# A hybrid-attention layer: the last two latent heads by token halves, and three token tiles of the output projection among the last values

## The chip, the cores and the metric

The kernel runs on one core of one Trainium2 chip. The metric is the device time of one execution in microseconds (us), from the chip's own clock. The core has a matrix engine (TensorE, PE in the profile, with PEld for its weight loads), three elementwise engines (VectorE is DVE, ScalarE is ACT, GpSimd is POOL) and SyncE (SP), which here only issues DMA transfers. Every engine works through its own instruction list in the order in which it was written down, and waits on semaphores for the others. TensorE multiplies a 128-row stationary matrix by up to 512 moving columns and adds into PSUM, a memory of eight banks of 128 x 512 floats. The granted clock of TensorE that the profile shows is a share of its full speed.

## The reference

The kernel computes one encoder layer for 1024 tokens of width 1024, in float32. What matters here is the end of the mixer and the beginning of the channel part:

```python
q = rmsnorm(...); k = rmsnorm(...)          # 8 latent heads, q and k of 96, v of 64
o_mla = mla_attention(q, k, v)              # chunk-causal: a 64-token chunk sees all chunks up to its own
o_ca = chunk_attention(cq, ck, cv, rel_bias)  # 8 band heads of 64, a band of 9 chunks
mixed = jnp.dot(jnp.concatenate([o_mla, o_ca], axis=-1), w_out)
x = x + g_a[:, None, :] * mixed
h = modulate(rmsnorm(x, g_mlp_norm), sh_m, sc_m)
u = causal_dwconv(jnp.dot(h, w_up), conv_w, conv_b)
gate, val = jnp.split(u, 2, axis=-1)
x = x + g_m[:, None, :] * jnp.dot(jax.nn.silu(gate) * val, w_down)
```

So the output projection of a 128-token tile needs the attention outputs of all 16 heads for those tokens, and the norm needs a whole row of the result.

## The kernel before, in words

**Precision.** A float32 product is made of three faster ones. Each operand is split into a high part and the remainder (hi_of, lo_of, lines 77 and 84): hi x hi, hi x lo and lo x hi are added in PSUM (lines 154 to 156, and 1075 to 1077 for the channel part).

**Attention.** The heads are worked through in units. A unit is one head and one half of the queries (g = 0 or 1, 512 tokens, four query tiles). There are 16 units of band heads and then 16 of latent heads, named by (group, head, half); the latent ones run in the order (group 0 or 1, head 0 to 3, half 0, 1). For each query tile, TensorE makes the scores (line 771) into a PSUM bank pair of the tag S, VectorE takes the row minimum (789, 790), ScalarE the exponential with its row sum (797), VectorE the reciprocal (799, 800), POOL the scaled high part (line 73) and VectorE the low part (819), both in 16 bits. SP then issues DMA transposes of them (831), and TensorE multiplies by the values (859). Values are done for two query tiles at a time, three tiles behind the scores (DEPTH). In the second half of a latent head a tile has 640 to 1024 keys, in the first 128 to 512. At the end of a unit ScalarE and VectorE divide and combine (868, 869) into a tile om, and SP stores it to oT_d in DRAM (873; for the last unit, the store is held and written down behind the first loads of the next stage, 871).

**Fillers.** Among the units the kernel runs independent work in small steps, paced by a debt of estimated cost (pace, fill_step, need). The last one, "oca" (f_oca), is the output projection of the band heads: it loads and splits half of w_out, makes a partial sum for each token tile ("oc", lines 154 to 156), and stores it to part_d. It is called to completion behind the last unit.

**Output projection.** load_wo loads (667) and splits the other half of w_out. o_load(t) loads the latent heads' outputs of a tile from oT_d (ol, line 1017), ScalarE makes the high part oh (77) and POOL the low part, in place in ol (84). For each tile, 24 matmuls go into a bank pair "op" of the pool psB; there are three such pairs. VectorE adds the partial sum pa (1134), multiplies by the gate gabc (1135) and adds x (1136); SP stores the result x1 (1137); ScalarE squares it (1138), POOL takes the reciprocal root (119, 120), and VectorE scales the row (1143). Loads of pa (1110), x (1114) and gabc (1117) come through SP, as do those of the first channel weights wu (1086), whose parts wa, wb, wd and wf ScalarE (77) and POOL (84) split. o_load(4) to o_load(7) each wait for a free buffer of a former tile.

**The channel part** starts with TensorE transposes of the normed rows (ht_ps, 1044; ScalarE, 1046, copies and modulates) and then builds sums of pages on VectorE (1172 to 1192), before its long run of matmuls from about 717 us.

**Order.** The program is written in the order above, but a list scheduler sets each engine's final order: it plays the instructions against estimated durations and takes high_priority offsets and issue_after (an instruction is written down behind another one) as its guides. The PSUM pool psA serves attention with the tags mm, S, T and others; psB, which has op and hT, is opened when psA is closed.

## Time and profile before

| | us |
|---|---|
| runs (three) | 1338.59, 1341.95, 1342.17 |
| median | 1341.95 |
| the profiled execution's own time | 1345.32 |
| its span, first to last instruction | 1343.5 |
| TensorE busy in the span | 1223.3 (91%) |
| VectorE busy | 1095.6 (82%) |
| ScalarE busy | 621.9 (46%) |
| POOL busy | 579.7 (43%) |
| mean granted TensorE clock | 0.948 |

The stages that matter, on the time axis of the profile: the last scores begin at 608.10, the last values at 621.17, the output projection's first matmul at 626.96 and its last at 674.05; the channel part's long run of matmuls starts at 717.5. Rows of the timeline give start, duration, engine, line, operation, and the tiles written and read, with the idle time of the engine in front and who ended it in square brackets. Rows of the chain give start, duration and the piece that the end of the program waited for. Shares of busy time are averages over stages with different limits, so the stretch of the change has to be read by itself.

### The profile page before, as it was taken

Reading aid. Unit: us, or ns where it says so; the run is one execution under the profiler, and the core shown is the slowest. Engines: PE = TensorE matmul, PEld = TensorE weight load, DVE = VectorE, ACT = ScalarE, POOL = GpSimd, SP = SyncE. Lnnn points to the kernel's source line nnn. Section 1 sums busy time; section 2 is a strip of 40 time slices with the busy share of each in tenths; the row PEclk is TensorE's granted clock in tenths of the full one; section 3 lists DMA queues with packets and bytes.
Section 4 is the critical chain, followed back from the end, with each engine's and each line's share of the span. In section 5 each row is a group of like instructions: output and inputs, shape, how many; then the busy total and the mean of one; then the engine's idle time right before and its main releaser. Section 6 shows DMA issues by size and latency. Waiting matters only on the chain.

```text
span 1343.5 us, 18697 instructions
## 1 busy us (share of the span) xinstructions
PE 1223.3 (91%) x6168; PEld 1002.6 (75%) x6168; DVE 1095.6 (82%) x1928; ACT 621.9 (46%) x1132; POOL 579.7 (43%) x610
## 2 busy tenths in 40 slices
PE   4899798998867798896988999999999999999998
PEld 3888587887655576774867888888888886888886
DVE  6977898864679987894989888899999997687667
ACT  4453555443556544552375444444434444433331
POOL 5474656565646763363725444444435431000000
PEclk9899798999797899997998999999999998999999
DMA  8415677944413486779901333333333326943441
GB/s 321 140 32 120 137 173 181 192 124 113 90 30 80 97 166 153 148 153 270 364 32 63 110 113 131 102 107 113 120 116 117 127 96 232 388 154 118 131 160 62
DMA packets 223689, 190.57 MB, mean 142 GB/s; under 512 B 148708, under 2 KB 166884, under 8 KB 223592
## 3 DMA queue, kind: packets, MB, share of 16 engines
q1 hardware_dynamic: 223592, 189.38, 49.5%
q8 instruction: 48, 0.79, 0.2%
q14 instruction: 49, 0.40, 0.1%
HBM read 117.24 MB, written 37.49 MB: 115 GB/s over the span
## 4 chain that ended last, share of the span: by engine, by line
PE 41%; DVE 10%; issue 3%; ACT 2%; DMA 1%; POOL 1%; SPq 0%; DVEq 0%; ACTq 0%; POOLq 0%
PE p L1075 7%; PE p L1077 7%; PE p L1076 7%; PE dnA_P L1404 2%; PE dnA_P L1406 2%; PE dnA_P L1405 2%; PE dnB_P L1406 1%; PE dnB_P L1405 1%; PE dnB_P L1404 1%; DVE u L1246 1%; DVE u L1247 1%; PE dnA L1404 1%; PE op L154 1%; PE dnA L1406 1%; PE dnA L1405 1%
## 5 line engine op out<-in xcount | busy, mean ns | idle before, releaser
L77 ACT ACTIVATE dnP<-dnr 128x1024 fp32r<-128x1024 f32 x73 | 77.5, 1064 | 117.1 <-PE dnA_P L1406 46.4
L1378 DVE TENSOR_TENSOR dnP<-dnr,dnP 128x1024 fp32r<-128x1024 f32 x72 | 87.9, 1223 | 52.5 <-ACT dnP L77 52.5
L73 POOL TENSOR_SCALAR hlm<-Pm,rim 128x512 f16<-128x512 f32 (+3 forms) x96 | 69.3, 732 | 79.8 <-DVE rim L800 21.8
L84 POOL TENSOR_TENSOR wf<-wu,wf 128x512 fp32r<-128x512 f32 x22 | 39.3, 1789 | 116.3 <-ACT wf L77 106.8
L1246 DVE SCALAR_TENSOR_TENSOR u<-c,cvp,u 128x1023 f32<-128x1023 f32 x44 | 65.0, 1519 | 27.8 <-ACT u L1245 27.8
L73 POOL TENSOR_SCALAR hlc<-Pc,ric 128x640 f16<-128x640 f32 (+2 forms) x64 | 49.7, 780 | 61.1 <-ACT Pc L797 15.4
L819 DVE SCALAR_TENSOR_TENSOR hlm<-Pm,rim,hlm 128x512 f16<-128x512 f32 (+3 forms) x96 | 66.7, 706 | 10.3 <-POOL hlm L73 10.1
L797 ACT ACTIVATE Pc<-sc,mc 128x640 f32<-128x640 f32 (+2 forms) x64 | 42.1, 658 | 53.5 <-DVE mc L786 30.6
L1245 ACT ACTIVATE u<-c,cvp 128x1024 f32<-128x1024 f32 x44 | 52.3, 1237 | 28.7 <-DVE c L1338 19.5
L84 POOL TENSOR_TENSOR wb<-wu,wb 128x512 fp32r<-128x512 f32 x22 | 38.5, 1751 | 61.6 <-ACT wb L77 55.5
L797 ACT ACTIVATE Pm<-sm,mm 128x128 f32<-128x128 f32 (+3 forms) x64 | 47.1, 736 | 38.4 <-DVE mm L790 21.1
L1247 DVE SCALAR_TENSOR_TENSOR u<-c,cvp,u 128x1022 f32<-128x1022 f32 x44 | 64.8, 1510 | 0.0
L859 PE MATMUL pvm<-PTm,vt 128*128 128x256 f16 (+1 forms) x320 | 46.6, 298 | 15.4 <-DMA PTm<-hlm 10.7
L819 DVE SCALAR_TENSOR_TENSOR hlc<-Pc,ric,hlc 128x640 f16<-128x640 f32 (+2 forms) x64 | 50.4, 790 | 8.8 <-POOL hlc L73 8.2
L154 PE MATMUL ipq<-wq_s,hT 128*128 128x256 f32 x192 | 56.1, 295 | 0.0
L155 PE MATMUL ipq<-wq_s,hT 128*128 128x256 f32 x192 | 56.0, 293 | 0.0
L859 PEld LDWEIGHTS <-vt 128*128 128x128 f16 x320 | 32.0, 110 | 31.5 <-DMA PTm<-hlm 15.0
L156 PE MATMUL ipq<-wq_s,hT 128*128 128x256 f32 x192 | 55.4, 289 | 0.0
L77 ACT ACTIVATE wc<-ws 128x512 fp32r<-128x512 f32 x21 | 13.3, 632 | 86.0 <-DVE ws L1094 86.0
L1406 PE MATMUL dnA_P<-dnP 128*128 128x512 f32 x132 | 51.3, 389 | 0.0
L1405 PE MATMUL dnA_P<-dnP 128*128 128x512 f32 x132 | 51.3, 389 | 0.0
L1404 PE MATMUL dnA_P<-dnP 128*128 128x512 f32 x132 | 51.2, 389 | 0.0
(434 smaller groups left out, 4429.6 us busy)
## 6 DMA issues: line engine op xcount, KB each, us to landing
wu<-w_up SPq DMA_DIRECT2D x44, 512.0 KB, 3.5
dnr<-g_d SPq DMA_DIRECT2D x73, 256.0 KB, 2.8
aw<-w_ada SPq DMA_DIRECT2D x48, 256.0 KB, 3.6
g_d<-u SPq DMA_DIRECT2D x22, 512.0 KB, 3.0
dnr<-w_down SPq DMA_DIRECT2D x44, 256.0 KB, 5.4
adaw<-w_ada_a SPq DMA_DIRECT2D x16, 512.0 KB, 6.5
x<-x SPq DMA_DIRECT2D x16, 512.0 KB, 9.0
g_d<-gs SPq DMA_DIRECT2D x22, 256.0 KB, 2.7
```

What stands on the lines that cost most here:

```text
L73: pool.tensor_scalar(o, i, s, 1.0, op0=MUL, op1=MUL)
L77: act.activation(o, i, AF.Copy)
L797: act.activation(pr[:, :n], sv, AF.Exp, bias=m[:], scale=-1.0, accum_out=rsum[:, 0:1])
L819: dve.scalar_tensor_tensor(hl[:, w:2 * w], pp, ri[:], hl[:, :w], op0=MUL, op1=SUB)
L859: last = pe.matmul(dst, u.vst(j), mov, start=(x == 0), stop=(x == len(todo) - 1), skip_group_check=True)
L1075: pe.matmul(pt, sh, pg[:, 0], start=(k == 0 and not add), stop=False, skip_group_check=skip)
L1076: pe.matmul(pt, sh, pg[:, 1], start=False, stop=False, skip_group_check=skip)
L1077: last = pe.matmul(pt, sl, pg[:, 0], start=False, stop=(k == 3), skip_group_check=skip)
L1378: r = f(*a, **k)
L1404: pe.matmul(pt, sh, w[:, 0, 0], start=start, stop=False, skip_group_check=add)
L1405: pe.matmul(pt, sh, w[:, 1, 0], start=False, stop=False, skip_group_check=add)
L1406: pe.matmul(pt, sl, w[:, 0, 0], start=False, stop=stop, skip_group_check=add)
```

## The change

Three things are changed together:

1. The last two latent heads are ordered by token halves: (2,0), (3,0), (2,1), (3,1) of group 1, where it was (2,0), (2,1), (3,0), (3,1). When (3,0) is done, all heads are finished for tokens 0 to 511, which are tiles 0 to 3 of the output projection. One key page of unit (1,3,1) moves into another buffer for it, and the stores of the last two units' outputs are both held and written down behind the first four ol loads.
2. The band heads' filler "oca" is called to completion in front of the last three score tiles (N_OCA) instead of behind all units, which also lets the other half of w_out be loaded and split earlier.
3. The products of tiles 0, 1 and 2 (op_product) go into banks of the attention's own pool: tile 0 into two banks of the tag mm, tiles 1 and 2 into pairs of the tag S. The last two query tiles' values, values(7), are written down behind the product of tile 1 (N_OP). psA is closed, and psB opened, behind the add of tile 2. The add of tile 0 is done in two halves.

In the instruction lists that come of it, ScalarE has the first three conversions oh in front of the exponentials of the last unit's tiles 6 and 7, and POOL the four low parts among that unit's high parts; VectorE has the adds of tiles 0, 1 and 2 in front of the x add of tile 0, and ScalarE the squares of x0 and x1 both in front of wa's conversion.

```diff
--- before.py
+++ after.py
@@ -38,6 +38,8 @@
 GRP = 2
 GSTEP, LAG = 2, 4
 NPRE = 10
+N_OCA = 3
+N_OP = 1
 DEPTH = 3
 OFF_S, OFF_P, OFF_V = 400, 200, 200
 P_BUFS, HL_BUFS, TB = 3, 4, 1
@@ -705,7 +707,7 @@
             act.activation(hi[:rows], pt[:rows], AF.Copy)
             dve.tensor_tensor(lo[:rows], pt[:rows], f32(hi[:rows]), op=SUB)
             return hi, lo
-        pg = at.tile([P, 2, 512], F32R, name=name, tag=tag, bufs=bufs)
+        pg = at.tile([P, 2, 512], F32R, name=name, tag=tag, bufs=bufs) if bufs else pgtile([P, 2, 512], F32R, name)
         act.activation(pg[:rows, 0], pt[:rows], AF.Copy, scale=gain)
         dve.scalar_tensor_tensor(pg[:rows, 1], pt[:rows], gain, f32(pg[:rows, 0]), op0=MUL, op1=SUB)
         return pg
@@ -867,7 +869,7 @@
                     inv = vscale[u.vs][1]
                     act.activation(dst[r0], u.pv[r1], AF.Copy, scale=inv[r1])
                     dve.scalar_tensor_tensor(dst[r0], u.pv[r0], inv[r0], dst[r0], op0=MUL, op1=ADD)
-                    if final:
+                    if u in units[-2:]:
                         held.append(lambda: sp.dma_start(u.dst_d[r0, u.g * 512:(u.g + 1) * 512], dst[r0]))
                     else:
                         anchor["om"] = sp.dma_start(u.dst_d[r0, u.g * 512:(u.g + 1) * 512], dst[r0]).ins
@@ -917,7 +919,7 @@
 
         def prep():
             q = qk_page(lambda j: mq[gr, (4 * g + j) // 2][:, j % 2, hh, :], f"mq{gr}{hh}_{g}", QK, "Q", 2, None)
-            k = qk_page(lambda j: mk[gr, (4 * g + j) // 2][:, j % 2, hh, :], f"mk{gr}{hh}_{g}", QK, "K", 3, gk_m[:QK])
+            k = qk_page(lambda j: mk[gr, (4 * g + j) // 2][:, j % 2, hh, :], f"mk{gr}{hh}_{g}", QK, "K", 0 if (gr, hh, g) == (1, 3, 1) else 3, gk_m[:QK])
             pages[gr, hh, g] = (q, k)
         u = Unit(f"m{gr}{hh}", 0, QK,
                  lambda: (pages[gr, hh, g][0], [pages[gr, hh, i][1] for i in range(g + 1)]),
@@ -979,9 +981,12 @@
             fill_step()
     first = [anchor["pe"]]
     units = [ca_unit(p, g, o) for p in range(4) for g in range(2) for o in range(2)]
-    units += [mla_unit(gr, hh, g) for gr in range(2) for hh in range(4) for g in range(2)]
+    units += [mla_unit(0, hh, g) for hh in range(4) for g in range(2)]
+    units += [mla_unit(1, hh, g) for hh, g in ((0, 0), (0, 1), (1, 0), (1, 1), (2, 0), (3, 0), (2, 1), (3, 1))]
     tiles = [(u, i) for u in units for i in range(4 * u.g, 4 * u.g + 4)]
     for n in range(len(tiles) + DEPTH):
+        if n == len(tiles) - N_OCA:
+            need(["oca"])
         if n < len(tiles):
             u, i = tiles[n]
             if i % 4 == 0:
@@ -992,7 +997,7 @@
             u, i = tiles[n - DEPTH]
             if i % 4 == 1:
                 need(u.needv)
-            if i % 2:
+            if i % 2 and n < len(tiles) + DEPTH - 1:
                 pace(u.values(i), R_CA if u.band else R_MLA)
     need(["oca"])
     for _ in side[0]:
@@ -1020,17 +1025,36 @@
 
     for t in range(4):
         o_load(t)
+    opt = {}
+
+    def op_product(t, outs):
+        for n in range(2):
+            for i, k in enumerate(range(4)):
+                for x, (a, b) in enumerate(((oh, 0), (oh, 1), (ol, 0))):
+                    last = pe.matmul(outs[n], a[t][:, k], wo[n][k][:, b], start=(i == 0 and x == 0), stop=(i == 3 and x == 2))
+        opt[t] = outs
+        return last.ins
+
+    early_ = {}
+    half = [ps.tile([P, 512], F32, name=f"op0_{n}", tag="mm", bufs=2) for n in range(2)]
+    op_last = op_product(0, [p[:] for p in half])
+    for t in range(1, 3):
+        pt = ps.tile([P, 1024], F32, name=f"op{t}", tag="S", bufs=2)
+        x = op_product(t, [pt[:, :512], pt[:, 512:]])
+        early_[t] = pt
+        if t <= N_OP:
+            op_last = x
+    with tc.issue_after(op_last):
+        units[-1].values(7)
     with tc.issue_after(anchor["ol"]):
-        held[0]()
+        for f in held:
+            f()
     att.__exit__(None, None, None)
     att_pg.__exit__(None, None, None)
-    psA.__exit__(None, None, None)
     gbp = tc.tile_pool(name="gB", bufs=1, side="right", reuse_waits="tile")
     gb = gbp.__enter__()
     xpool = tc.tile_pool(name="xp", bufs=1, side="left", reuse_waits="tile")
     xp = xpool.__enter__()
-    psB = tc.tile_pool(name="psB", bufs=1, space=PSUM, reuse_waits="tile")
-    ps2 = psB.__enter__()
     gmbc = xp.tile([P, D], F32, name="gmbc")
     hpl = tc.tile_pool(name="h2p", bufs=1, side="left", reuse_waits="tile")
     h2p = hpl.__enter__()
@@ -1124,14 +1148,22 @@
         x_load(t)
     sp.dma_start(cvp[:], I["pack"][:, C_CV:])
     for t in range(NT):
-        pt = ps2.tile([P, 1024], F32, name=f"op{t}", tag="op", bufs=3)
-        for n in range(2):
-            gemm3(pt[:, n * 512:(n + 1) * 512],
-                  [(oh[t][:, k], ol[t][:, k], wo[n][k][:, 0], wo[n][k][:, 1]) for k in range(4)])
+        if t not in opt:
+            pt = ps2.tile([P, 1024], F32, name=f"op{t}", tag="op", bufs=3)
+            op_product(t, [pt[:, :512], pt[:, 512:]])
         if t + 4 < NT:
             o_load(t + 4)
         pa, x1 = op_[t], ox[t]
-        dve.tensor_tensor(pa[:], pa[:], pt[:], op=ADD)
+        if t == 0:
+            for n in range(2):
+                sl = slice(n * 512, (n + 1) * 512)
+                dve.tensor_tensor(pa[:, sl], pa[:, sl], opt[0][n], op=ADD)
+        else:
+            dve.tensor_tensor(pa[:], pa[:], pt[:] if t > 2 else early_[t][:], op=ADD)
+        if t == 2:
+            psA.__exit__(None, None, None)
+            psB = tc.tile_pool(name="psB", bufs=1, space=PSUM, reuse_waits="tile")
+            ps2 = psB.__enter__()
         dve.tensor_tensor(pa[:], pa[:], gabc[:], op=MUL)
         dve.tensor_tensor(x1[:], x1[:], pa[:], op=ADD)
         sp.dma_start(x1_d[t], x1[:])
```

## The prediction

> **What bounds the kernel now.** I read the page first, then the chain of work that ended last from 590 to 720 us, then the engines' timelines over that stretch, and last table rows of short windows.
>
> ```profile
> span 1343.5 us, 18697 instructions
> PE 1223.3 (91%) x6168; PEld 1002.6 (75%) x6168; DVE 1095.6 (82%) x1928; ACT 621.9 (46%) x1132; POOL 579.7 (43%) x610
> ```
>
> TensorE is busy 91% of the span, so a change of the order can win only in the 9% in which it is not. The change acts where attention ends and the output projection begins. TensorE's timeline there (start, duration, instruction, idle time before and who ended it):
>
> ```profile
> 610.31 1.96 PE L859 MATMUL pvm<-PTm,vt 128*128 128x256 f16 x12 [1.58 <-DVE om L869]
> 615.05 2.75 PE L859 MATMUL pvm<-PTm,vt 128*128 128x256 f16 x12 [2.79 <-DVE om L869]
> 621.17 3.35 PE L859 MATMUL pvm<-PTm,vt 128*128 128x256 f16 x16 [3.37 <-DMA PTm<-hlm]
> 626.96 0.50 PE L154 MATMUL op<-wo,oh 128*128 128x512 f32 x1 [2.44 <-ACT oh L77]
> ```
>
> The four gaps are 1.58 + 2.79 + 3.37 + 2.44 = 10.2 us: the holes that early products could fill. What the end hangs on behind them, the chain says (start, duration, piece):
>
> ```profile
> 620.46 3.79 DMA wor<-w_out
> ...
> 635.48 1.23 DVE pa L1134
> ...
> 639.26 1.16 ACT pa L1138 x2
> ...
> 649.53 2.28 POOL ol L84
> 651.85 0.50 PE op L156
> ...
> 674.05 0.24 PE op L156
> ...
> 678.93 2.32 DVE x L1136
> ```
>
> The reader is to see that the chain does not stay on TensorE. It goes from the load that follows the last transpose through, the first product, VectorE's add (635.48), the square of x0 (until 640.42), then POOL until ol4's low part (651.81), and only then into the product of tile 4. From there TensorE runs to 674.29, and VectorE is behind: its last x add ends 681.25, 6.96 later. Windows (length, busy time of PE, weight loads, DVE, ACT, POOL; granted clock, DMA share, GB/s):
>
> ```profile
> 612.00:624.00 12.00, 5.78 (x29) 3.51 (x27) 4.30 (x8) 1.39 (x3) 2.40 (x3) 0.50 0.85 175
> 628.00:632.00 4.00, 4.00 (x12) 2.83 (x11) 0.00 (x0) 1.03 (x2) 3.99 (x4) 0.60 1.03 405
> 640.00:650.00 10.00, 10.00 (x45) 8.27 (x45) 9.39 (x6) 4.28 (x9) 9.25 (x8) 1.00 1.04 396
> 690.00:717.00 27.00, 22.38 (x111) 17.89 (x109) 25.56 (x43) 19.81 (x35) 3.25 (x1) 0.99 0.00 0
> ```
>
> 45 matmuls in 10.00 us is 0.22 to 0.23 each, so a tile of 24 is 5.4 us. DMA is full from 628 on (share 1.03 and 1.04), the clock of the first tile's matmuls was 0.60 over 4 us, which lost 4 x 0.4 = 1.6 us, and 690 to 717 is VectorE's (25.56 of 27).
>
> **The change part by part.**
>
> *The three products.* 72 matmuls x 0.225 = 16.2 us leave the stretch behind the values and go in front of or among the last values. The holes hold 10.2, and the tail gets longer (next step), so tiles 0 and 1 are covered; tile 2 ends about 634 (below), where it now ends near 626.96 + 1.6 + 3 x 5.4 = 644.8. The later part of the stage gains from this only if tile 4 starts earlier too.
>
> *What stands in front of the last scores' work.* The order of TensorE, ScalarE and POOL now has the four o_load conversions among the last unit's tiles: on ScalarE oh0 to oh2 in front of the exps of score tiles 6 and 7, on POOL all four low parts in front of the last high parts of the probabilities. Both engines are in order, so they now wait for the ol landing. SP's queue and POOL:
>
> ```profile
> 617.72 2.68 SPq L831 DMA_TRANSPOSE PTm<-hlm  x2
> 620.46 1.08 SPq L667 DMA_DIRECT2D wor<-w_out  x2
> 621.63 2.02 SPq L1017 DMA_DIRECT2D ol<-oT_d  x4
> 623.75 1.34 SPq L1117 DMA_DIRECT2D gabc<-ga_d  x1
> 625.19 1.33 SPq L1110 DMA_DIRECT2D pa<-part_d  x3
> 627.09 0.46 SPq L871 DMA_DIRECT2D oT_d<-om  x1
> 627.59 0.58 SPq L1110 DMA_DIRECT2D pa<-part_d  x1
> 628.22 0.91 SPq L1114 DMA_DIRECT2D x<-x  x2
> ```
>
> ```profile
> 626.99 5.00 POOL L84 TENSOR_TENSOR ol<-ol,oh 128x512 fp32r<-128x512 f32 x4 [9.21 <-ACT oh L77]
> ...
> 641.30 1.30 POOL L84 TENSOR_TENSOR wa<-wu,wa 128x512 fp32r<-128x512 f32 x1
> 642.54 2.28 POOL L84 TENSOR_TENSOR wb<-wu,wb 128x512 fp32r<-128x512 f32 x1
> ```
>
> And the ol tiles' DMA, from issue to landing:
>
> ```profile
> DMA to landing us min/median/max: 4.8/7.2/8.5
> ```
>
> The first four loads now go out behind the transposes of unit (2,1), ahead of (3,1)'s. The four low parts are 5.00 us of POOL, and a conversion of ScalarE's of that size is 0.62:
>
> ```profile
> 640.31 0.62 ACT L77 ACTIVATE wa<-wu 128x512 fp32r<-128x512 f32 x1
> ```
>
> Lower bound of the delay of the last transpose: 0, if all of it fits idle time (POOL had 9.21 in front of that row) and the landing is early. Upper bound: 5.00 + 3 x 0.62 behind a landing of 7.2 instead of 4.8, together 9.3. I take 5.5, nearest to the 5.00 row with a little for the wait: SP is free of transposes at 625.9 instead of 617.72 + 2.68 = 620.40. The last values, which ended at 621.17 + 3.35 = 624.5, then end at 630.0, and what is left of tile 2, some 4.4, ends at 634.4. Splitting the output weights and the oca fillers in front of the last scores costs nothing: the chain's 3.79 of wor behind the last transpose goes away with it. It cannot be won for itself, since the ol landing and the first pa stood right behind it. Swapping the order of (3,0) and (2,1) changes no count of instructions.
>
> *Loads.* gabc, the pa, the om stores, the x and wu follow the transposes on SP. The x loads stand behind the store of the last om too, which waits for the last values and VectorE. So gabc goes out at 626.3 (+2.5), the first pa at 627.7 (+2.5), x at 631.2 (+3.0), wu as much later. But wor (0.5 MB) and the ol (1.0 MB) have gone ahead of the full stretch; at 405 GB/s they were 3.7 us of it. So landings move by 3.0 - 3.7 = -0.7, about 0:
>
> ```profile
> x<-x SPq DMA_DIRECT2D x5, 512.0 KB, 9.0
> pa<-part_d SPq DMA_DIRECT2D x4, 512.0 KB, 8.0
> ```
>
> x0 before: 628.22 + 9.0 = 637.2; after 636.5. pa0 before 633.2; after 627.7 + 8.0 - 3.7 = 632.0.
>
> *VectorE.* The adds of pa0 (halves), pa1 and pa2 and three gabc products now come ahead of x0's add; pa2 waits for tile 2's product.
>
> ```profile
> 645.83 1.21 DVE L1134 TENSOR_TENSOR pa<-pa,op 128x1024 f32<-128x1024 f32 x1
> 647.07 2.33 DVE L1135 TENSOR_TENSOR pa<-pa,gabc 128x1024 f32<-128x1024 f32 x1
> ```
>
> At 1.22 each: pa2 634.4 to 635.6, two gabc to 638.1, x0 to 639.3, x1 to 640.6. ScalarE now has the squares of x0 and x1 both in front of wa: 640.6 + 1.16 + 0.62 = 642.4 for POOL's start on wa's low part, 1.1 later than 641.30. Queued behind it on POOL: wb, wd, wf, then ol4's low part, for which tile 4 waits. That is 651.81 - 641.30 = 10.5 us now. Bounds: all five low parts at 1.30 with 0.8 for the small ops between them, an estimate, 7.3; all at 2.28 with 2 for the small ops 13.4. VectorE's list in this stretch (pa3, x2, a gabc, x3, two norms) is about as full as now, so I keep 10.5: tile 4 starts at 652.9, 1.05 later than 651.85.
>
> The rows show the contention: VectorE's gabc product, with both inputs in SBUF, took 2.33 beside POOL, while the add with one input in PSUM kept 1.21. The Trainium skill, page "SBUF — State Buffer", section "Who interferes with whom", says the same: a VectorE instruction with two SBUF inputs contends with GpSimd's reads, one with a PSUM input does not. By it the five low parts are dear only while such instructions last; in the end that VectorE waits for tile 4 from about 650, the last low part would be cheap, and the sum would come out 1.0 lower, 1341.7.
>
> *TensorE's new wait.* Tile 3 waits for VectorE's add of tile 1 (its banks) and ends about 640; then TensorE stands 12.5 us until 652.9. So the 16 us that the early products took out of the stage come back as this wait. VectorE's wait too: pa4 has to wait for tile 4's end at 658. The restart: the clock of 0.60 stood behind the last gaps and lost 1.6; in 612 to 624, with gaps of 2.79 and 3.37, it was 0.50. I charge the same 1.6 at 652.9; bounds 0 and 2 (4 us at 0.50). The Trainium skill, page "TensorE: Matmul & The Clock Gate", section "Part 1: The HAM clock gate", has the clock halved after an idle window of some 3.4 us and back after as long a busy one, which speaks against the change: 1.7 by that rule, an estimate.
>
> *The end of the stage.* Tiles 4 to 7 take 674.29 - 651.85 = 22.4, so the last ends 652.9 + 22.4 + 1.6 = 676.9 (+2.6). VectorE has no backlog then: pa7, gabc, x7 at 1.22 to 2.32 and one norm are 5.1 instead of 6.96 (-1.9; bounds 0 and -2.2). Then 690 to 717 follows as it is, VectorE's work unchanged.
>
> *Sum.* 1.05 + 1.6 - 1.9 = +0.75. The profiled execution's own 1345.32 would be 1346.1; it lies 3.4 above the median 1341.95, so for the median 1342.7.
>
> **The rivals.**
> *A, the tail stretches (slower).* If the ol landing takes the 7.2 of the row and not some 4 in the emptier DMA before 628, ScalarE and POOL stand with the last exps and high parts queued behind them, and the transposes end at 629.5 or later instead of 625.9. For: both queues are in order, and TensorE's products wait for the same landing in front of values. Against: DMA moved 175 GB/s in 612 to 624, less than half of full. The point: each us beyond 625.9 goes through the loads, the squares and POOL to tile 4 one for one: at 629.9, 1342.7 + 4.0 = 1346.7, and more above. It decides from 629.2.
> *B, POOL is quicker (faster).* If the transposes end by 623.5, the wu are there by 639, and the low parts run at 1.30: 641 + 7.3 = 648.3, tile 4 starts 4.6 earlier than in my sum, less of a wait: 1342.7 - 4.6 - 1.0 = 1337. For: VectorE's work for tiles 0 to 2 is done in a lump earlier. Against: ScalarE has a second square ahead of wa.
> *C, contention at its worst.* All five low parts at 2.28: 13.4 instead of 10.5, 1342.7 + 2.9 = 1345.6.
>
> **How the numbers follow.** 0.3% is 4.0 us, about what a measurement of this kernel can tell from no change. The forecast has 0.42, A 0.24, B 0.24, C 0.10. The forecast's own range is 1339 to 1346, mostly same. Faster is B and a little of the forecast's low side, 0.26; slower A, half of C's upper side and a little of the forecast, 0.31; the rest, 0.43, same. The range: low 1335 is B with no half clock (1.6); high 1350 is A with the last transpose at 633, beyond the 9.3 bound of the delay by what the loads may add.
>
> **What would show it.** In the profile after: the last L831 ending at 625 to 627; tiles 0 and 1 among the last values; a wait of 10 to 13 us on TensorE ended by POOL ol L84 at about 653; the granted clock down to 0.50 for some 3 us behind it; the last x add about 5 us behind the last op matmul. Wrong if TensorE's wait is short (B), if the last transpose is past 629 (A), or if the 690 to 717 stretch changes its length.

## The result and the profile after

The changed kernel is slower: 1351.89 us in the median (1347.23 to 1355.47, 8 runs), against 1342.99 us (1338.59 to 1347.01, 8 runs) of the kernel before beside it. The ratio is 1.0058, 95% interval 1.0042 to 1.0074, which is 7.8 us (5.6 to 9.9); the medians lie 8.9 apart. 1342.7 was forecast, inside "no change"; the range ended at 1350. The profiled execution of the changed kernel took 1350.41 us, 5.1 more than that of the kernel before.

```profile
PE 1222.0 (91%) x6168; PEld 1002.7 (74%) x6168; DVE 1094.5 (81%) x1929; ACT 622.5 (46%) x1132; POOL 573.1 (42%) x610
```

All engines are as busy as before (TensorE 1222.0 against 1223.3), so the time is waiting, not work. TensorE's timeline after the change, the last values and the rows behind them that have an idle time in brackets (start, duration, instruction, idle time before it and who ended it):

```profile
631.06 0.94 PE L861 MATMUL pvm<-PTm,vt 128*128 128x256 f16 x8
638.72 0.84 PE L1034 MATMUL op<-wo,oh 128*128 128x512 f32 x2 [2.53 <-DVE pa L1162]
650.42 1.22 PE L1034 MATMUL op<-wo,oh 128*128 128x512 f32 x2 [4.39 <-ACT oh L79]
656.21 0.79 PE L1034 MATMUL op<-wo,ol 128*128 128x512 f32 x1 [4.57 <-POOL ol L86]
```

The early products do fill the holes: from 612 to 624 TensorE was busy 12.00 of 12.00 us (window below) where it had been busy 5.78. What they leave behind is three waits of 2.53 + 4.39 + 4.57 = 11.5 us further on. SP's queue shows what is late in front of them:

```profile
611.89 1.06 SPq L1022 DMA_DIRECT2D ol<-oT_d  x2
613.05 5.15 SPq L833 DMA_TRANSPOSE PTm<-hlm  x3
618.65 0.46 SPq L873 DMA_DIRECT2D oT_d<-om  x1
620.92 8.22 SPq L833 DMA_TRANSPOSE PTm<-hlm  x5
629.49 0.34 SPq L1141 DMA_DIRECT2D gabc<-ga_d  x1
630.10 1.79 SPq L1134 DMA_DIRECT2D pa<-part_d  x4
633.54 0.46 SPq L873 DMA_DIRECT2D oT_d<-om  x1
634.04 1.09 SPq L1138 DMA_DIRECT2D x<-x  x2
```

The last transpose ends at about 629.1, 8.7 later than the 620.40 of before; the gate, partial-sum and x loads stand behind it, 5 to 6 us late. POOL's list, which tile 4 waits for, is late by the same:

```profile
646.32 1.27 POOL L86 TENSOR_TENSOR wa<-wu,wa 128x512 fp32r<-128x512 f32 x1
647.55 2.25 POOL L86 TENSOR_TENSOR wb<-wu,wb 128x512 fp32r<-128x512 f32 x1
...
651.97 2.24 POOL L86 TENSOR_TENSOR wf<-wu,wf 128x512 fp32r<-128x512 f32 x1
...
654.90 1.26 POOL L86 TENSOR_TENSOR ol<-ol,oh 128x512 fp32r<-128x512 f32 x1
```

wa's low part begins at 646.32 instead of 641.30 (+5.0), ol4's ends at 656.16 instead of 651.81. Tile 4 goes on at 656.21 instead of 651.85 (+4.4), and the projection's last matmul ends at 680.20 instead of 674.29 (+5.9). The difference of the two, 1.5, is the clock. Windows (length; busy time of PE, weight loads, VectorE, ScalarE, POOL; granted clock, DMA share, GB/s):

```profile
600.50:609.80 9.30, 5.82 (x34) 4.59 (x33) 8.89 (x17) 4.41 (x10) 4.75 (x5) 1.00 0.99 205
612.00:624.00 12.00, 12.00 (x57) 9.42 (x56) 8.82 (x16) 5.52 (x9) 9.27 (x11) 0.87 0.78 161
...
650.40:656.20 5.80, 1.22 (x2) 0.50 (x2) 5.67 (x4) 1.67 (x3) 5.64 (x5) 0.50 1.05 409
656.20:660.20 4.00, 3.99 (x11) 3.18 (x12) 0.51 (x1) 0.63 (x1) 3.83 (x5) 0.58 1.06 385
```

The clock is 0.58 in the 4 us behind the long wait, which loses 4 x 0.42 = 1.7.

### The profile page after: what moved, and what is told of

Same layout as the page of the kernel before. It is cut to its first block, busy times and chain, and to the rows that moved or that the text cites. A ratio compares the mean times of both kernels' runs of the same rounds, so it can differ in the third digit from the quotient of the medians.

```text
span 1348.6 us, 18696 instructions
## 1 busy us (share of the span) xinstructions
PE 1222.0 (91%) x6168; PEld 1002.7 (74%) x6168; DVE 1094.5 (81%) x1929; ACT 622.5 (46%) x1132; POOL 573.1 (42%) x610
## 4 chain that ended last, share of the span: by engine, by line
PE 30%; DVE 17%; issue 4%; ACT 2%; DMA 2%; POOL 1%; SPq 0%; DVEq 0%; ACTq 0%; POOLq 0%
PE p L1099 3%; PE p L1101 3%; PE p L1100 3%; PE op L1034 3%; DVE u L1279 3%; DVE u L1278 3%; PE dnA_P L1436 2%; PE dnA_P L1437 2%; PE dnA_P L1438 2%; PE dnB_P L1437 1%; PE dnB_P L1438 1%; PE dnB_P L1436 1%; ACT u L1277 1%; DVE we L86 1%; DVE ws L1118 1%
## 5 line engine op out<-in xcount | busy, mean ns | idle before, releaser
L75 POOL TENSOR_SCALAR hlm<-Pm,rim 128x512 f16<-128x512 f32 (+2 forms) x96 | 69.9, 737 | 82.4 <-DVE rim L802 21.3
L86 POOL TENSOR_TENSOR wf<-wu,wf 128x512 fp32r<-128x512 f32 x22 | 40.1, 1823 | 116.2 <-ACT wf L79 112.6
L821 DVE SCALAR_TENSOR_TENSOR hlm<-Pm,rim,hlm 128x512 f16<-128x512 f32 (+2 forms) x96 | 67.6, 715 | 8.4 <-POOL hlm L75 8.2
L86 POOL TENSOR_TENSOR wb<-wu,wb 128x512 fp32r<-128x512 f32 x22 | 38.8, 1764 | 62.7 <-ACT wb L79 49.5
L861 PE MATMUL pvm<-PTm,vt 128*128 128x256 f16 (+1 forms) x320 | 44.2, 287 | 10.6 <-DMA PTm<-hlm 10.6
L1034 PE MATMUL op<-wo,oh 128*128 128x512 f32 x128 | 43.3, 418 | 6.9 <-ACT oh L79 4.4
```

The costliest lines, as they stand in the source:

```text
L75: pool.tensor_scalar(o, i, s, 1.0, op0=MUL, op1=MUL)
L86: (pool if eng == "p" else dve).tensor_tensor(o, i, f32(hi), op=SUB)
L821: dve.scalar_tensor_tensor(hl[:, w:2 * w], pp, ri[:], hl[:, :w], op0=MUL, op1=SUB)
L1034: last = pe.matmul(outs[n], a[t][:, k], wo[n][k][:, b], start=(i == 0 and x == 0), stop=(i == 3 and x == 2))
```

## The experiments

Profiles of the same code differ by a few us ahead of the last two heads (their start lies between 567.4 and 573.7 on the axes of the profiles). So all times in the table count from a mark in each profile: the start of the first exponential of the last two latent heads. "Goes on" is the first low-part matmul of tile 4, which waits for POOL, and "c" is ScalarE's first copy of the channel part's result. The ratios are those of the measured times to the kernel before, run on the same chip. Five kernels that differ only behind the attention (after, e6, e9, e11, e15) have their last transposes between 57.9 and 58.6, so a difference of some 0.7 between two profiles tells nothing.

| run | last exponential | last transpose ends | tile 4 goes on | last projection matmul ends | c | ratio [95%] |
|---|---|---|---|---|---|---|
| before | 40.1 | 49.0 | 80.4 | 102.8 | 145.0 | 1 |
| after | 49.1 | 58.1 | 85.2 | 109.2 | 151.8 | 1.0058 [1.0042, 1.0074] |
| e1_order | 53.0 | 60.9 | | 112.2 | 154.4 | 1.0059 [1.0039, 1.0079] |
| e2_oca | 44.4 | 53.7 | | 107.3 | 149.5 | 1.0044 [1.0023, 1.0065] |
| e3_order_oca | 49.2 | 58.4 | | 108.0 | 150.2 | 1.0025 [1.0010, 1.0040] |
| e4_behind | 49.9 | 58.6 | | 108.8 | 151.0 | 1.0025 [1.0010, 1.0040] |
| e5_conv | 48.8 | 56.5 | | 116.0 | 158.2 | 1.0069 [1.0050, 1.0088] |
| e6_tile4 | 49.2 | 58.6 | 81.6 | 108.1 | 150.4 | 1.0033 [1.0012, 1.0055] |
| e9_ol4 | 49.7 | 58.0 | 89.0 | 107.5 | 152.5 | 1.0071 [1.0046, 1.0096] |
| e10_oldorder_ol4 | 44.9 | 54.1 | | 110.1 | 152.4 | 1.0033 [1.0013, 1.0052] |
| e11_tile4b | 49.7 | 58.6 | 81.5 | 106.9 | 152.1 | 1.0025 [1.0008, 1.0042] |
| e12_scores | 49.7 | 57.8 | | 109.3 | 151.9 | 1.0048 [1.0032, 1.0064] |
| e13_wolo | 48.0 | 60.9 | | 113.4 | 156.0 | 1.0068 [1.0051, 1.0084] |
| e14_all | 45.1 | 58.1 | 80.4 | 105.9 | 151.0 | 1.0022 [1.0004, 1.0040] |
| e15_splits | 49.8 | 57.9 | 81.6 | 106.4 | 149.6 | 1.0027 [1.0011, 1.0043] |
| e16_splits_behind | 48.9 | 57.6 | | 107.8 | 153.5 | 1.0043 [1.0025, 1.0061] |
| e17_splits_all | 46.1 | 58.3 | 82.4 | 106.9 | 150.1 | 1.0037 [1.0018, 1.0055] |
| e18_before_splits | 40.2 | 49.0 | | 101.9 | 147.7 | 1.0029 [1.0011, 1.0047] |

(In e9 the wait had moved to tile 5, so "goes on" is the first low-part matmul of tile 5 there: 661.73 on its own axis.)

### What makes the last transposes late: order, filler or products

Theory, from the result: the tail is stretched by the attention-output conversions that stand in front of the last exponentials. Rivals: the new order of the units, the earlier filler, or the products themselves. The first two experiments do one part of the change on the kernel before.

```diff
 e1_order (on before)
-    units += [mla_unit(gr, hh, g) for gr in range(2) for hh in range(4) for g in range(2)]
+    units += [mla_unit(0, hh, g) for hh in range(4) for g in range(2)]
+    units += [mla_unit(1, hh, g) for hh, g in ((0, 0), (0, 1), (1, 0), (1, 1), (2, 0), (3, 0), (2, 1), (3, 1))]
 e2_oca (on before)
     for n in range(len(tiles) + DEPTH):
+        if n == len(tiles) - 3:
+            need(["oca"])
```

> The kernel before with the new order of the last two heads alone (and the key page's buffer and nothing else). Counted from the first exp of the last two heads, the last transpose ended 49.0 us later before, 58.1 later in the change, 58.4 later with the order and the early filler but without early products. Theory O (the order puts eight long tiles in a row, and the scores of the last unit stand in line behind values that wait for transposes): 56 to 59 here too, and the time is 2 to 5 us above the kernel before's. Theory F (the early oca filler and the weights' splits in front of the last scores make the delay): 49 to 52 here, and the time is the kernel before's within 2 us.

> The kernel before with the oca filler called to completion in front of the last three score tiles, and nothing else. Theory O: the last transpose stays at 49 to 51 us behind the first exp of the last two heads, the waits for wor behind it are gone, and the time is 0 to 3 us below the kernel before's. Theory F: the last transpose is 3 to 9 us later, and the time 2 to 5 us above.

The order alone puts the last transposes 11.9 later (60.9 against 49.0), the filler alone 4.7 later. That is past theory O's 56 to 59 for e1, and within theory F's 3 to 9 for e2. Both kernels are slower, 1.0059 and 1.0044.

The two that follow have both parts: e3 without any early product, e4 with the products in the same banks but written down behind the last values.

```diff
 e3_order_oca: the two edits above together, on before
 e4_behind (on after)
-            if i % 2 and n < len(tiles) + DEPTH - 1:
+            if i % 2:
...
+    behind = tc.issue_after(trail[-1])
+    behind.__enter__()
     half = [ps.tile([P, 512], F32, name=f"op0_{n}", tag="mm", bufs=2) for n in range(2)]
...
+    behind.__exit__(None, None, None)
-    with tc.issue_after(op_last):
-        units[-1].values(7)
```

> The new order of the units and the early oca filler, as in the change, but no early products: all eight tiles' products stand behind the values, in psB. In the changed kernel the last transpose ended at 629.1 where it ended at 620.4 before. Theory P (products in front of the values hold TensorE, and the transposes wait for TensorE to free their buffers): the last transpose ends at 624 to 626, tile 4 is in time behind tiles 0 to 3, and the time is 1343 to 1346. Theory Q (the ol conversions stand in front of the last exps and high parts and wait for the ol landing): the last transpose still ends at 628 to 629, and the time is 1350 to 1354, since tiles 0 to 2 come 10 us later than in the change. Theory R (POOL's list in front of tile 4 costs the 4.4 us, whatever the tail does): as Q or P in the tail, but no long wait on TensorE before tile 4.

> The changed kernel with the three early products, in the same banks, written down behind the last values instead of in front. The ol conversions stay in front of the last exps. Theory P: values and transposes are free of the products, the last transpose ends at 626 or before instead of 629.1, loads, squares and POOL come 3 us earlier, and the time falls by 2 to 4 us below the changed kernel's. Theory Q: the last transpose stays at 628 to 629, and the time is as in the changed kernel within 2 us, since the wait of tile 4 takes up what the products lose.

The last transposes are as late as in the changed kernel (58.4 and 58.6 against 58.1), with no product in front of the last values. So the products are not the cause; order and filler make the delay without them. The conversions are not ruled out by these two runs: the list scheduler put them early here as well. In e3 POOL makes the low parts in front of the last high parts:

```profile
613.51 2.49 POOL L84 TENSOR_TENSOR ol<-ol,oh 128x512 fp32r<-128x512 f32 x2 [1.85 <-ACT oh L77]
```

Order and filler do not add up either. With the old order the filler costs 4.7; with the new one the last transposes come 2.5 earlier with it than without it (58.4 against 60.9). The traces suggest why: in e1 the low parts of the output weights stand among the last unit's tiles (VectorE has them at 613.15, 616.39, 620.88 and 622.98), and in e3 ahead of that unit, where VectorE had time to spare in e1 (below).

Both kernels are at 1.0025, less slow than the changed one: products in front of the last values win nothing over products behind them. Theory Q of both runs was right on the transposes and wrong on the time.

The next takes the conversions out of the way of the last unit: ScalarE's high parts wait behind the last exponential, POOL's low parts behind the last high part of the probabilities.

```diff
 e5_conv (on after)
-        hi_of("a", oh[t][:], f32(ol[t][:]))
-        lo_of("p", ol[t][:], f32(ol[t][:]), oh[t][:])
+        with tc.issue_after(anchor["exp"]):
+            hi_of("a", oh[t][:], f32(ol[t][:]))
+        with tc.issue_after(anchor["hi"]):
+            lo_of("p", ol[t][:], f32(ol[t][:]), oh[t][:])
```

> The changed kernel with the conversions of ol0 to ol3 written down behind the last exp on ScalarE and behind the last high part on POOL. Theory Q: exps and high parts no longer wait for the ol landing, the last transpose ends 2 to 4 us earlier than 629.1, and the time falls by 2 to 4 us below the changed kernel's, although the products start later. Theory P: products that now wait for conversions at 622 hold the values longer still; the last transpose is no earlier, and the time is the same or up to 3 us longer.

The last transposes come 1.6 earlier (56.5), no more. The conversions that I had charged with the whole delay carry at most 1.6 of 9.1. (In the changed kernel's trace all four of ScalarE's conversions, not three, stand in front of the exponentials of tiles 6 and 7.) The kernel is no faster (1.0069): the products, and the last values behind them, now wait for the late conversions, and the last matmul ends at 116.0.

Where the rest lies is seen in ScalarE's exponentials, first of before, then of after (with its first conversion), then of e1 (start, duration, shape):

```profile
590.90 1.10 ACT L797 ACTIVATE Pm<-sm,mm 128x1024 f32<-128x1024 f32 x1
592.66 0.37 ACT L797 ACTIVATE Pm<-sm,mm 128x128 f32<-128x128 f32 x1
...
601.50 0.79 ACT L797 ACTIVATE Pm<-sm,mm 128x640 f32<-128x640 f32 x1 [1.00 <-PE pvm L859]
```

```profile
600.56 1.12 ACT L799 ACTIVATE Pm<-sm,mm 128x1024 f32<-128x1024 f32 x1
...
609.79 0.79 ACT L799 ACTIVATE Pm<-sm,mm 128x640 f32<-128x640 f32 x1 [4.89 <-DVE mm L792]
...
614.25 0.63 ACT L79 ACTIVATE oh<-ol 128x512 fp32r<-128x512 f32 x1 [2.64 <-DMA ol<-oT_d]
...
620.12 1.12 ACT L799 ACTIVATE Pm<-sm,mm 128x1024 f32<-128x1024 f32 x1 [0.49 <-DVE mm L792]
```

```profile
600.80 1.11 ACT L797 ACTIVATE Pm<-sm,mm 128x1024 f32<-128x1024 f32 x1 [2.78 <-DVE mm L790]
...
608.21 0.79 ACT L797 ACTIVATE Pm<-sm,mm 128x640 f32<-128x640 f32 x1 [5.64 <-DVE sm L789]
```

Before, unit (3,0), with its four short tiles, ran between the last exponential of (2,1) at 590.90 and the first of (3,1) at 601.50, a gap of 10.6. In the new order (3,0) is done ahead of (2,1), which pushes (2,1)'s last exponential to 600.56, 9.7 later; and the gap up to (3,1) is still 9.2, with nothing of (3,0) in it. From there the last unit takes as long as before (609.79 to 620.12, against 601.50 to 611.50). So the short unit had cost next to nothing in its old place.

The first exponential of (3,1) settles what makes the delay. It comes 30.1 behind the mark before and 38.8 after, so 8.7 of the 9.1 are there already; the first conversion (614.25) and the first early product (616.48) come behind it. With the order alone (e1) it comes at 38.1, 8.0 later than before, and the first conversion of e1 too comes behind it (613.01); with the filler alone (e2) it comes at 33.6. So the order makes the delay.

What fills the gap is less clear. In the gap of after, VectorE is full: 8.89 of 9.30 busy in the first window above. In e1 it is not: 4.68 of 7.41 (600.80 to 608.21), with TensorE's clock at 0.52. VectorE's timeline in the gap of after:

```profile
603.45 0.74 DVE L712 SCALAR_TENSOR_TENSOR mk<-mk_ps,gk_m,mk 96x512 fp32r<-96x512 f32 x1
604.11 1.65 DVE L86 TENSOR_TENSOR wo<-wor,wo 128x512 fp32r<-128x512 f32 x2
...
606.34 1.28 DVE L86 TENSOR_TENSOR wo<-wor,wo 128x512 fp32r<-128x512 f32 x2
...
608.92 1.61 DVE L792 TENSOR_REDUCE mm<-sm 128x1 f32<-128x640 f32 x2
```

In front of the row minimum of (3,1)'s first tiles stand the low parts of (2,1)'s last probabilities, a key page, and 1.65 + 1.28 = 2.93 of the output weights' low parts, which the early filler brought there. In front of the scores stand values that wait for transposes. Three runs tried these two.

```diff
 e12_scores (on after): values of (2,1)'s tiles 4 and 5 behind (3,1)'s scores
+                with tc.issue_after(trail[-1]) if u is units[-2] and i == 5 else contextlib.nullcontext():
+                    cost = u.values(i)
+                pace(cost, R_CA if u.band else R_MLA)
 e13_wolo (on after): the weights' low parts on VectorE behind the last row minimum
-            lo_of(le, w[:, 1], raw[:], w[:, 0])
+            with tc.issue_after(anchor["dve"]) if le == "v" else contextlib.nullcontext():
+                lo_of(le, w[:, 1], raw[:], w[:, 0])
 e14_all (on after): both, and e11's edit (below)
```

> The changed kernel with one move on TensorE: the scores of (3,1)'s first two tiles stand in front of the values of (2,1)'s first pair, instead of half behind them. Theory S (the 9.2 us between the exp of (2,1)'s last tile and that of (3,1)'s first come from scores in line behind values that wait for transposes): this gap falls to 5 to 7, and the last transpose is 2 to 4 us earlier than 58.1. Theory D (VectorE's list, with four low parts of the output weights and the low parts of the probabilities in front of the next row minimum, makes the gap): the gap stays at 8 to 9.2, and the last transpose within 1 of 58.1.

> The changed kernel with the four low parts of the second half of the output weights, 2.9 us of VectorE, written down behind the last row minimum. Theory D: the gap of 9.2 us falls by 2 to 3, the last exps are no longer behind the ol conversions, the last transpose is 3 to 6 us earlier than 58.1, and the time 2 to 5 us below the changed kernel's. Theory S: the gap stays within 1 us, and the last transpose within 2.

> The three moves together: tile 4's conversion early, the scores in front of the values, the weights' low parts behind the last minimum. If tail and tile 4 are the two causes, the mark at ScalarE's copy of c is at 143 to 146, and the time is the kernel before's or 1 to 2 us below. If the order of the units costs by itself whatever stands in the lists, the mark stays at 148 or above, and the time 2 us or more above.

One at a time they do next to nothing to the gap: it stays 9.0 with the scores moved (29.4 to 38.4) and 8.5 with the weights moved (29.6 to 38.1), and moving the weights alone makes the last transposes later (60.9). Both together shorten it to 5.4, as ScalarE's rows of e14 show:

```profile
597.87 1.12 ACT L800 ACTIVATE Pm<-sm,mm 128x1024 f32<-128x1024 f32 x1
603.24 0.80 ACT L800 ACTIVATE Pm<-sm,mm 128x640 f32<-128x640 f32 x1 [1.03 <-DVE sm L792]
```

The last exponential comes at 45.1 instead of 49.1, yet the last transpose ends at 58.1, as in the changed kernel: the work pushed out of the gap comes back between the last exponential and the last transposes. VectorE now makes the weights' low parts there and has the last reciprocal's tile ready only at 620.16, 6.3 behind the exponential's end, and POOL has the conversions in front of the last high parts:

```profile
616.52 4.72 POOL L1027 TENSOR_TENSOR ol<-ol,oh 128x512 fp32r<-128x512 f32 x3
621.23 1.35 POOL L75 TENSOR_SCALAR hlm<-Pm,rim 128x512 f16<-128x512 f32 x2
```

So the conversions hold the last transposes by some 1.1 there, from 620.16 to 621.23, and VectorE's list makes most of the rest. These two moves do not get back what the order lost, and c (151.0) and ratio are as forecast for the case that the order costs by itself.

### What makes tile 4 late: POOL's list

The low parts of the four channel weights stand in POOL's list in front of tile 4's conversion. Three edits give tile 4 another place: e6 puts tile 4's conversions in front of all four splits and of all squares and roots, e11 only in front of the splits and of the squares from tile 2 on, and e9 instead has tile 4's input loaded in front of the x loads.

```diff
 e6_tile4, e11_tile4b (on after): the four splits, taken out of their old place, stand behind tile 4's conversion
+        if t == 0:
+            with tc.issue_after(anchor["oh"]), tc.issue_after(anchor["lo"]):
+                wa0, wb0 = split(raw0[0][:, :512], "wa0"), split(raw0[0][:, 512:], "wb0")
+                w21 = split(raw0[1][:, :512], "wd_0")
+                w22 = split(raw0[1][:, 512:], "wf0")
...
 e9_ol4 (on after)
+    o_load(4)
     sp.dma_start(gabc[:], ga_d[:])
...
 e10_oldorder_ol4: e9 with the old order of the units, products behind the last values
```

> The changed kernel with tile 4's conversion (oh4 and its low part) in front of the first squares and of wa, wb, wd and wf on ScalarE and POOL; nothing else is moved. In the changed kernel tile 4 waits for POOL until 656.2, and TensorE stands 4.39 + 4.57 us before it. Theory R: tile 4 starts when ol4 lands, at 646 to 648, TensorE has no wait over 3 us there, and the time falls by 6 to 9 us, to about that of the kernel before. Theory P or Q alone (the end hangs on the late loads, not on this list): tile 4 starts earlier, but VectorE or the loads take over, and the time falls by less than 3 us.

> The changed kernel with tile 4's conversion in front of wa, wb, wd and wf and of the squares from tile 2 on, on ScalarE and POOL; ol4's load stays at its place, and the squares and roots of tiles 0 and 1 stay in front, so that no norm waits for a root. Counted from the first exp of the last two heads, the first page sum of the channel part (ScalarE's copy of c) was at 145.0 us before, 151.8 in the change, 150.4 when all squares were moved. Theory R (the loss is TensorE's and VectorE's wait for tile 4): tile 4 starts 4 to 6 us earlier than in the change, VectorE's wait of 6.42 falls to 2 or less, the mark is at 146 to 148, and the time falls by 4 to 6. Theory L (the late tail and the loads behind it set the end): tile 4 starts earlier, VectorE waits elsewhere, the mark is at 150 to 152, and the time falls by less than 3.

> The changed kernel with ol4 loaded in front of the x loads and converted in front of the first squares and of wa; the squares and roots of tiles 0 and 1 stay in front of wa, so that the norms don't wait as they did with all squares moved. Theory R (the late loads cost little by themselves, and the time is lost where TensorE and then VectorE wait for tile 4): no wait for ol4 on TensorE, VectorE's waits of 6.42 and 2.23 us for tiles 4 and 5 fall to under 2 together, and the time falls by 6 to 9 us below the changed kernel's, to the kernel before's or 1 to 2 below it. Theory L (the late tail sets the end, since the first pa lands when the transposes are done): the waits go elsewhere, to the loads of x4, pa4 or the roots, and the time falls by 2 to 4.

> The same early load and conversion of tile 4, and the early filler, with the old order of the last two heads; the three products go into the attention's banks, behind the last values, since (3,0) is stored only shortly before the last transposes. Theory O: the last transpose is at 49 to 51 us, and the time is 0 to 4 us below the kernel before's. Theory F: the last transpose is at 53 or later, and the time is the kernel before's or above.

In e6 and e11 tile 4 goes on at 81.6 and 81.5 instead of 85.2. The ratio falls to 1.0033 [1.0012, 1.0055] and 1.0025 [1.0008, 1.0042], against 1.0058 [1.0042, 1.0074]: by the ratios POOL's list was worth 0.33%, or 4.4 us, in e11, where the two intervals just touch. But the last matmul does not come 3.7 earlier, only 1.1 and 2.3. TensorE's waits in e11:

```profile
653.80 1.15 PE L1034 MATMUL op<-wo,oh 128*128 128x512 f32 x2 [3.44 <-ACT oh L1023]
...
663.91 0.50 PE L1034 MATMUL op<-wo,ol 128*128 128x512 f32 x1 [1.56 <-POOL ol L1024]
```

A wait remains, now for the high part, and one comes up in front of tile 5 (663.91), whose low part stands behind the displaced splits.

e9 failed by its own edit. SP's queue in e9:

```profile
635.84 0.45 SPq L873 DMA_DIRECT2D oT_d<-om  x1
641.23 0.37 SPq L1022 DMA_DIRECT2D ol<-oT_d  x1
641.64 0.98 SPq L1138 DMA_DIRECT2D x<-x  x2
```

Tile 4's load reads what the store of the last unit's output writes. That store went out at 635.84 and landed at 641.21, and the load stood in SP's queue until then (641.23). The x loads stood behind it and went out 5.8 later, counted from the mark, than in the changed kernel. So e9 says nothing of POOL's list. e10 has the same load; with the old order and the early filler its last transposes come at 54.1, which agrees with e2 (53.7) and says no more than e2.

The last four were made to settle whether POOL's list is the limit for tiles 4 to 7 together: the four splits behind tile 7's conversion, on the changed kernel (e15), on e4 (e16), with e14's two moves (e17), and on the kernel before (e18).

```diff
 e15_splits (on after; e16 on e4_behind, e17 on e12 and e13 together, e18 on before)
+        if t == 3:
+            with tc.issue_after(anchor["oh"]), tc.issue_after(anchor["lo"]):
+                wa0, wb0 = split(raw0[0][:, :512], "wa0"), split(raw0[0][:, 512:], "wb0")
+                w21 = split(raw0[1][:, :512], "wd_0")
+                w22 = split(raw0[1][:, 512:], "wf0")
```

> The changed kernel, with the low and high parts of the four feed-forward pages (wa, wb, wd, wf) placed behind tile 7's attention-output conversion instead of in front of tile 4's, squares left where they are. Theory (GpSimd's list makes tiles 4 to 7 late; once it is clear nothing else is): tile 4 starts at about 81 us after the mark (85.2 in the changed kernel), no TensorE wait in front of tile 5 over 0.5 us, last projection matmul at 102 to 104 us (109.2), ratio 1.000 to 1.002. Rival (the late attention tail and the loads behind it set these tiles): tile 5's wait of 1.2 to 2 us stays as in the three runs that moved only tile 4, last matmul 106 to 108 us, ratio 1.002 to 1.004. The four pages then come later, before the first feed-forward products: if they were short of time there, ScalarE's first copy of c would still come 42 us behind the last matmul but a wait for a page would show behind it.

> The same move of the four pages, in the version whose three early products stand behind the last values. It has no TensorE gap to fill by early products in the attention, so the products start at 62 us after the mark. Theory (the list alone, early products worth little): last projection matmul at 105 to 107 us (108.8 without the move), ratio 1.001 to 1.002, 2 us behind the run with products early. Rival (loads and tail set it): 108 to 109 us, ratio 1.0025 as without the move.

> The first kernel of this set, with in addition the scores of the last tile-unit in front of the values of the unit before, and the four low parts of the projection's weights behind the last minimum. Theory (list clear, tail 4 us shorter up to the last exp): last projection matmul at 101 to 103 us, ratio 0.998 to 1.000. Rival (loads and tail): 105 to 106 us as in the run with tile 4 alone moved, ratio 1.002.

> The kernel before with only the four pages' parts behind tile 7's conversion. If GpSimd's list delayed the projection's later tiles there too, its last matmul comes earlier than 102.8 us after the mark (100 to 102) and the ratio is 0.997 to 0.999. If it was covered there, nothing moves: 102.8 us, ratio 0.999 to 1.001. The pages being late for the feed-forward part would show as a ratio above 1.001 with the last matmul unmoved.

e15 has tile 4 going on at 81.6, as in e11, and no wait in front of tile 5 any more. The rival had that wait stay. Still the last matmul ends at 106.4, in the range of the rival (106 to 108), not of the theory (102 to 104). TensorE's waits in e15:

```profile
637.57 0.70 PE L1034 MATMUL op<-wo,oh 128*128 128x512 f32 x2 [2.33 <-DVE pa L1170]
649.13 1.22 PE L1034 MATMUL op<-wo,oh 128*128 128x512 f32 x2 [5.88 <-ACT oh L1023]
651.04 0.80 PE L1034 MATMUL op<-wo,ol 128*128 128x512 f32 x1 [0.69 <-POOL ol L1024]
```

and the windows behind them:

```profile
651.00:655.00 4.00, 3.96 (x9) 3.14 (x10) 1.37 (x2) 0.63 (x1) 2.34 (x3) 0.50 1.04 409
655.00:659.00 4.00, 4.00 (x18) 3.21 (x17) 0.39 (x2) 0.63 (x1) 0.60 (x1) 0.86 1.07 381
```

With POOL's list cleared in front of tile 4, TensorE waits 5.88 for the high part, and ScalarE, which makes it, waits for the load:

```profile
648.45 0.63 ACT L1023 ACTIVATE oh<-ol 128x512 fp32r<-128x512 f32 x1 [0.59 <-DMA ol<-oT_d]
```

That load was issued at 639.09 and landed 9.3 later. SP's queue shows the store that it reads from:

```profile
632.60 0.45 SPq L873 DMA_DIRECT2D oT_d<-om  x1
```

The store landed at 639.06, and the loads ahead of tile 4's in the queue had gone out at 639.04, so neither let it go earlier. Tile 4's first low-part matmul then comes 1.2 later than in the kernel before, and the clock behind the wait is 0.50 and 0.86, which loses 4 x 0.50 + 4 x 0.14 = 2.6. Together 3.8; the last matmul is 3.6 later than before. So with the list cleared, what is left is the late load and the half clock. Store and x loads both follow the last values, and these the last transposes; but no run separated the tail from the loads, since none had the new order with an early tail.

e17 has nearly the same last matmul (106.9, ratio 1.0037) although its last exponential is 3.7 earlier: nearer to the rival (105 to 106) than to the theory (101 to 103). e16 falls between its two forecasts (107.8) and is no faster than e4, from which it differs only in the splits (1.0043 and 1.0025, intervals that overlap). Its last matmul comes 1.4 later than that of e15, which has the products early; the ratios of these two overlap as well. And the control e18 is slower than the kernel before, 1.0029, although its last projection matmul is 0.9 earlier. VectorE's timeline in e18 around that matmul:

```profile
668.83 2.31 DVE L1143 TENSOR_TENSOR pa<-pa,gabc 128x1024 f32<-128x1024 f32 x1
671.17 2.18 DVE L1144 TENSOR_TENSOR x<-x,pa 128x1024 f32<-128x1024 f32 x1
...
676.41 1.21 DVE L1142 TENSOR_TENSOR pa<-pa,op 128x1024 f32<-128x1024 f32 x1
```

Its last add of a partial sum starts 676.41 - 671.6 = 4.8 behind the last matmul (671.6 = 569.67 + 101.9), where the kernel before starts it at once; c comes 45.8 behind the matmul instead of 42.2. In their old place the splits had cost TensorE a wait of 0.54; moved behind tile 7 they run on POOL until 674.5, beside the last products of VectorE. Tile 6's gate product and x add took 2.31 and 2.18 there, where the kernel before has 1.22 and 1.23. That these collide is read from the two timelines and was not tested by itself.

No kernel here beats the one before; the lowest of the changed ones, e14, is at 1.0022.

## Why the prediction was wrong

**The delay of the last transposes** is the step that failed: the order of the units was put at nothing ("changes no count of instructions"), and the whole delay was charged to the conversions in front of the last exponentials and high parts. It was to be 5.5 (bounds 0 and 9.3). It measured 8.7 on the profiles' axes, 9.1 from the mark, inside the bounds but from another cause. With the order alone the first exponential of (3,1) is 8.0 later (e1), before any conversion; the conversions are 1.6 at most (e5). That the swap changes no count was true and beside the point: it took the short unit out of a gap that stays 9.2 long without it. And "costs nothing" of the early filler was wrong by 4.7 with the old order (e2), though with the new one the tail is 2.5 shorter with it (e3 against e1).

What follows came out as rival A had it: last transposes 629.1 instead of 625.9 is +3.2, tile 4 goes on at 656.21 instead of 652.9, +3.3. That the two match so well is luck in part: POOL's list began 3.9 later than forecast and was 0.7 shorter. Rival A named the place; its time (1345.9 by its rule at 629.1, +4.0) is still short of the measured 5.6 to 9.9. And its reason, a late landing of the attention outputs, is not the cause: their first load was issued at 610.70, behind the first exponential of (3,1) at 609.79, which was late already.

**VectorE's backlog at the end** (-1.9) was misread. It was taken from the 6.96 between the last matmul and the last x add, as if VectorE came with work left over. A row of the profile before says otherwise, and two of the changed kernel agree with it:

```profile
674.31 1.22 DVE L1134 TENSOR_TENSOR pa<-pa,op 128x1024 f32<-128x1024 f32 x1 [1.03 <-PE op L156]
```

```profile
680.24 1.22 DVE L1162 TENSOR_TENSOR pa<-pa,op 128x1024 f32<-128x1024 f32 x1 [1.43 <-PE op L1034]
...
684.86 2.32 DVE L1168 TENSOR_TENSOR x<-x,pa 128x1024 f32<-128x1024 f32 x1
```

VectorE stood idle for 1.03 in front of the last add in the kernel before already. The 6.96 are tile 7's add, gate product and x add with two norms between them, and they are 6.98 after. There was nothing to gain. c came 42.2 behind the last matmul before and 42.6 after.

**The other steps.** The early products: covered, as predicted; the last values ended at 632.0 (630.0 forecast), and tile 2 behind them at 636.2 (634.4). The loads: pa0 was used from 634.89 (632.0 forecast), x was issued at 634.04 (631.2), both late by the tail. POOL: start 646.32 (642.4), and 646.32 to 656.16 is 9.8 for the list (10.5). ol4's low part took 1.26, where wb, wd and wf, beside VectorE products of two SBUF inputs, took 2.24 to 2.25. The Trainium skill, page "SBUF — State Buffer", section "Who interferes with whom", has a VectorE instruction with at most one SBUF input, outside the two-port modes, not contend with GpSimd, and by that the prediction had the last low part cheap. The trace agrees with 1.26 for it, though the norm that VectorE made beside it took 1.84, where the one at 656.88 in the kernel before took 0.74. The list came out 0.7 shorter, not enough to change the sign. TensorE's waits: 12.5 forecast, 11.5 measured, of which 2.53 stand in front of tile 3 already. The half clock: 1.6 forecast; tile 4's restart to the last matmul took 680.20 - 656.21 = 24.0 instead of 22.4, +1.6.

**The sum again**, with what was measured: tile 4 +4.4, clock +1.6, backlog 0, that is +6.0; the profiles have +5.9 at the last matmul, and the runs 5.6 to 9.9 in all. Forecast were +1.05, +1.6 and -1.9, so the late tail took 3.3 and the backlog 1.9 of the 5.2 between the two sums. Rival C (1345.6) did not come: POOL's list was shorter, not longer. Rival B needed transposes by 623.5.

What the parts cost is told by ratios: the order alone 1.0059 and the filler alone 1.0044, both together 1.0025 (e3, and e4 with its products behind the values); early products on top with POOL's list as it is 1.0058; with the list out of tile 4's way 1.0025 again (e11), 1.0027 (e15). No ratio shows a gain from the early products: the tiles behind them waited for POOL's list, and without it for the load and the clock.

**Open.** What fills the gap between (2,1) and (3,1) is known only so far that two moves together shorten it and neither does alone. e4 and the changed kernel differ by 0.33% in the runs, but their profiles by 0.8 us at c; behind c, where the two have the same code, the profiles differ by 2.8 more (623.0 against 625.8), so one profile each does not settle where the rest lies. In the same way e11's gain shows in its runs, but in its profile c is no earlier (152.1 against 151.8): theory R by the time, theory L by c.

## What to carry to other kernels

Before an item of work is moved forward, look whether it ran for nothing where it was: a short unit between two long ones can fill a gap which is nearly as long without it, and then the move pays for the unit a second time. Work done early is worth what the next step behind it gains, here nothing that the runs show, since tile 4 waited for a load and for another engine's list; so follow the first wait after the work that was moved, before counting the holes that it fills. And a distance between two engines' ends is no backlog unless the row at its head shows that the engine had no idle time there.

## What the runs showed of the hardware

A wait of some 2 us on TensorE can cost more than 1 us of clock behind it, and need not. The clock over 3.6 us behind the wait in front of tile 3, first in the changed kernel (a wait of 2.53), then in e15 (2.33):

```profile
638.70:642.30 3.60, 3.58 (x9) 2.82 (x10) 3.60 (x4) 0.00 (x0) 0.00 (x0) 0.56 1.03 420
```

```profile
637.57:641.17 3.60, 3.60 (x16) 3.01 (x17) 3.60 (x4) 0.00 (x0) 0.00 (x0) 1.00 1.03 420
```

The first lost 3.6 x 0.44 = 1.6, the second nothing, and TensorE did 9 matmuls in the one and 16 in the other. In front of the same tile, waits of 2.03, 2.18 and 2.48 were followed by 0.65, 0.53 and 0.58 (e6, e12, e11), and waits of 2.07 and 2.18 by 1.00 (e5, e9). Of the longer waits in that stretch of these profiles (560 to 690 us), from 2.7 us up, each was followed by 0.50 to 0.69. The loss of 1.6 was hidden in the changed kernel, since tile 4's wait stood behind tile 3 anyway; in e15 the loss behind tile 4's wait was 2.6 of the 3.6 that were left. The Trainium skill, page "TensorE: Matmul & The Clock Gate", section "Part 1: The HAM clock gate", has the halving follow an idle window of about 3.4 us; here 2.03 was enough in one run, and 2.33 was not in another.
